# Four weight buffers at four places: 48, 56, 72 and 80 bytes past a multiple of 128, instead of 64 for all

## The chip, the core and the metric

The kernel runs on one core of one Trainium2 chip. The metric is the time of one execution on the device in microseconds (us), the median of several runs. Five engines of the core work side by side and wait for each other through semaphores: TensorE (PE in the profile; its weight loads are listed as PEld), VectorE (DVE), ScalarE (ACT), GpSimd (POOL) and SyncE (SP), which here issues most of the transfers. The on-chip memory has 128 partitions; a tile lies at the same byte address in each of them, and "where a tile lies" below means this address within a partition.

## The reference, cut to what matters

Two layers of a decoder on 256 tokens with a width of 2048, all in float32. Every matrix product of a layer goes through the same piece of code in the kernel:

```python
for i in range(DEPTH):                      # DEPTH = 2
    a = rmsnorm(h, attn_norm[i])
    if i % 2 == 0:                          # 8 stick-breaking and 8 dilated heads
        h = h + sb_dilated_mixer(a, positions, w_in_even[i // 2], w_out_even[i // 2])
    else:                                   # 16 heads with forget gates
        h = h + fox_mixer(a, w_in_odd[i // 2], b_forget[i // 2], w_out_odd[i // 2])
    h = h + conv_ffn(rmsnorm(h, ffn_norm[i]), w_up[i], conv_w[i], conv_b[i], w_down[i])
    gate = sigmoid(rmsnorm(h, ple_norm[i]) @ w_ple_gate[i])
    h = h + gate * (p[i] @ w_ple[i])
return rmsnorm(h, final_norm)
```

The FFN has 5632 hidden features twice (gate and value), so `w_up` and `w_down` are the largest part of the weights.

## The kernel before, in words

All weights lie in the order in which they are used in one long array in the chip's main memory. They are cut into *units*: a unit is up to four k-tiles (128 rows each) of a 256 columns wide stripe of one weight matrix. A list of all units is made ahead (`_units`, L61), and transfers of 1 MB bring two units at a time into one of three raw buffers `wr` (`issue_group`, L150).

A float32 weight is used in two parts. `split_unit` (L169) takes the next unit, ScalarE copies it into a float32r tile as the high part (L176), and VectorE subtracts this high part from the raw value and writes the remainder as the low part (L177). Both parts lie in one tile `w` of 2048 elements per partition, ordered by k-tile, then part, then column. The pool hands out four such buffers in turn (L174). `unit` (L183) keeps three units split ahead (`LOOK = 3`) of the one that TensorE reads.

The activations lie in two large tiles `act` (with high and low part for each k-tile) that change roles, and `pact` for the layer's own embedding. `gemm_unit` (L207) makes 24 matmuls of one unit of four k-tiles: for each of the two 128-column halves, for each k-tile, the three products high x high, high x low and low x high (`PARTS`). The weights are the stationary operand (128 columns, 512 bytes a partition), the activations the moving one (256 tokens, 1024 bytes a partition). For the v projection (`gemm_v`, L240) the roles are exchanged: activations stationary, weights moving. Once, for the second layer's first heads, v and the forget gates are made together, with 272 columns (`gemm_vf`, L253).

The results go to tiles in the accumulation memory named by the product: psq, psk, psv (projections), pso (output projection), psu and psd (FFN up and down), psg (gate), psp (embedding), pse (last gate tile). The attention's own matmuls (`scs`, `sps`, `avp`) are put between the units by a small clock (`tick`, `defer`): a step is due some units after the one that it follows. They read other tiles in plain float32 or, for a few, in float32r.

Where things lie: pools are laid out in the order in which they are opened and used. Ahead of the weight buffers stand `act` twice, `pact` and a tile of 16 elements, `gap` (L117), that nothing reads or writes. The activations begin at a multiple of 128 bytes, and are multiples of 128 long; so the four weight buffers, the raw buffers behind them and `h` and `pl` all begin 64 bytes past a multiple of 128, and the buffers are 8192 bytes apart.

Of the kernel before, what the change touches and what calls it, by code (L numbers as in the profile page):

```python
# [11 lines left out]
F32R = mybir.dt.float32r  # L12
# [5 lines left out]
P = 128  # L18
# [86 lines left out]
def trunk(ctx: ExitStack, tc: tile.TileContext, xT, pT, pos, gains, conv, bf, cst, wst, out):  # L105
# [3 lines left out]
    apool = ctx.enter_context(tc.tile_pool(name="apool", bufs=1))  # L109
    wpool = ctx.enter_context(tc.tile_pool(name="wpool", bufs=1))  # L110
# [3 lines left out]

    bufs = [apool.tile([P, KT, 2, S], F32R, name=f"act{i}") for i in range(2)]
    pact = apool.tile([P, 2, 2, S], F32R, name="pact")
    apool.tile([P, 16], F32, name="gap")  # L117
    h = cpool.tile([P, KT, S], F32, name="h")
    pl = cpool.tile([P, KT, S], F32, name="pl")
# [28 lines left out]
    at = {"group": 0, "off": 0, "unit": 0, "tick": 0, "rows": 0}  # L148

    def issue_group():  # L150
        g = GROUPS[at["group"]]
        n = sum(u[3] * u[5] for u in g)
        if g[0][:2] == ("w_ple", 0):

            op = g[0][4] // 256
            raw = pl[:, 2 * op:2 * (op + len(g)), :].rearrange("p a s -> p (a s)")
        else:
            raw = wpool.tile([P, 2048], F32, name="wr", tag="wr", bufs=3)
        src = wst[at["off"]:at["off"] + P * n].rearrange("(p f) -> p f", p=P)
        nc.sync.dma_start(out=raw[:, :n], in_=src)  # L160
        at["off"] += P * n
        at["group"] += 1
        o = 0
        for u in g:
            m = u[3] * u[5]
            raws.append((u, raw[:, o:o + m].rearrange("p (k c) -> p k c", c=u[5])))
            o += m

    def split_unit():  # L169
        if not raws:  # L170
            issue_group()
        u, raw = raws.pop(0)
        kc, cw = u[3], u[5]
        w = wpool.tile([P, 2048], F32R, name="w", tag="w", bufs=4)  # L174
        w = w[:, :2 * kc * cw].rearrange("p (k s c) -> p k s c", s=2, c=cw)
        nc.scalar.copy(out=w[:, :, 0, :], in_=raw)  # L176
        nc.vector.tensor_sub(out=w[:, :, 1, :], in0=raw, in1=w[:, :, 0, :].bitcast(F32))  # L177
        at["unit"] += 1
        ready.append((u, w))
# [3 lines left out]
    def unit(kind, l, k0, c0):  # L183
        while len(ready) < LOOK and at["unit"] < len(UNITS):
            split_unit()
        u, w = ready.pop(0)
        assert (u[0], u[1], u[2], u[4]) == (kind, l, k0, c0), (u, kind, l, k0, c0)
        return u[3], w
# [458 lines left out]
    for l in range(DEPTH):  # L647
        st = {}
        if l == 0:
            split_unit()  # L650
            rest_of_start()
            for op in range(8):
                if op in (2, 4, 6):
                    for i in (op - 2, op - 1):
                        norm_parts(i, 0, X)
                ple_up(0, op)
            defer(1, lambda: norm_parts(6, 0, X))
            defer(2, lambda: norm_parts(7, 0, X))
            constants()
            for i in range(8):  # L660
                defer(3 + i, lambda i=i: norm_squares(i, tc.keep_in_program_order))
            norm_finish(True, 12, 14)
# [164 lines left out]
```

## Time and profile before

| what | value |
|---|---|
| median of 3 runs | 2423.63 us (2423.62 to 2424.76) |
| the profiled execution's own time | 2424.3 us |
| its span, first to last instruction | 2422.5 us |
| mean granted TensorE clock | 0.997 |
| matmuls in psu (up) and psd (down) | 8448 and 4224 |
| read from main memory | 452.86 MB, 188 GB/s over the span |

The page of the profile gives busy time by engine, the span in 40 slices, the chain of work that ended last, and the costliest groups of instructions. In a group's row stand the line, the engine, the operation, the names of output and inputs, the shapes and the count; then the busy time in us and the mean duration of one in ns; then the idle time of that engine just before them with what ended it. Matmuls are pipelined: one of 276 ns overlaps the next ones, so that the duration isn't the time that a matmul costs. The chain in order of time has rows of three parts, start, length and what ran, and as it has no overlap the length divided by the count is the step from one matmul to the next. The four weight buffers are used in turn, so a piece of 96 matmuls of the chain (one output tile) has gone through each of them once.

### The profile page before, as it was taken

The page shows a single profiled execution, that of the slowest core. Times are in us where ns is not written, and L with a number is a line of the kernel's source. Part 1 is how long each engine was busy: PE and PEld are TensorE (multiplying, and loading weights), DVE is VectorE, ACT ScalarE, POOL GpSimd, SP SyncE. Part 2 cuts the span into 40 slices and gives each one's busy share as a digit, 9 for nine tenths or more (in the row PEclk, how much of TensorE's full clock was granted, in tenths as well). Part 3 has the DMA queues.
Part 4 walks back from the last instruction along what each step waited for, and adds up shares of the span by engine and source line. Part 5 has one row for each costly group of instructions (what it writes and reads, how often), then busy time and mean ns, then how long its engine had stood idle before and what let it go on. Part 6 is the DMA issues. An engine that isn't in the chain of part 4 may idle for free.

```text
span 2422.5 us, 47951 instructions
## 1 busy us (share of the span) xinstructions
PE 2408.5 (99%) x21006; PEld 2403.4 (99%) x21006; DVE 1581.7 (65%) x2066; ACT 1230.9 (51%) x1546; POOL 5.9 (0%) x13
## 2 busy tenths in 40 slices
PE   9999999999999999999999999999999999999998
PEld 9999999999999999999999999999999999999998
DVE  7666766776567657767755555667665776567666
ACT  6654455554355445555554444555544554455554
POOL 0000000000000000000000000000000000000000
PEclk9999999999999999999999999999999999999998
DMA  7444455555555555555555454555555555555553
GB/s 287 170 175 170 175 182 192 192 194 192 197 197 196 187 196 192 193 187 203 185 184 175 167 182 162 198 191 194 192 192 193 194 196 190 202 192 187 187 201 122
DMA packets 66818, 458.05 MB, mean 189 GB/s; under 512 B 7552, under 2 KB 7840, under 8 KB 16944
## 3 DMA queue, kind: packets, MB, share of 16 engines
q1 hardware_dynamic: 66576, 454.93, 53.0%
q8 instruction: 164, 2.69, 0.4%
q14 instruction: 46, 0.38, 0.1%
q0 software_dynamic: 32, 0.06, 0.0%
HBM read 452.86 MB, written 2.10 MB: 188 GB/s over the span
## 4 chain that ended last, share of the span: by engine, by line
PE 99%; DVE 0%; DMA 0%; ACT 0%; issue 0%; SPq 0%; POOLq 0%; DVEq 0%; ACTq 0%
PE psu L214 40%; PE psd L214 20%; PE psk L214 7%; PE psq L214 7%; PE pso L214 7%; PE psv L248 7%; PE psg L214 7%; PE avp L525 1%; PE psv L261 0%; PE psp L214 0%; PE pse L725 0%; PE scs L481 0%; PE sps L516 0%; PE avp L527 0%; DMA h<-in_x 0%; PE scs L479 0%
## 5 line engine op out<-in xcount | busy, mean ns | idle before, releaser
L177 DVE TENSOR_TENSOR w<-wr,w 128x1024 fp32r<-128x1024 f32 (+2 forms) x874 | 1045.9, 1198 | 688.0 <-ACT w L176 683.6
L176 ACT CAST w<-wr 128x1024 fp32r<-128x1024 f32 (+2 forms) x874 | 903.2, 1034 | 1064.2 <-PE psu L214 353.4
L214 PE MATMUL psu<-act,w 128*128 128x256 f32 x8448 | 959.5, 276 | 0.0
L214 PEld LDWEIGHTS psu<-act,w 128*128 128x128 f32 x8448 | 958.3, 188 | 0.0
L214 PE MATMUL psd<-act,w 128*128 128x256 f32 x4224 | 479.7, 276 | 0.0
L214 PEld LDWEIGHTS psd<-act,w 128*128 128x128 f32 x4224 | 479.2, 188 | 0.0
L214 PE MATMUL psk<-act,w 128*128 128x256 f32 x1536 | 183.6, 279 | 0.0
L214 PE MATMUL psq<-act,w 128*128 128x256 f32 x1536 | 182.6, 279 | 0.9 <-DVE w L177 0.9
L214 PEld LDWEIGHTS psq<-act,w 128*128 128x128 f32 x1536 | 178.5, 188 | 1.4 <-DVE w L177 1.1
L214 PEld LDWEIGHTS psk<-act,w 128*128 128x128 f32 x1536 | 179.0, 188 | 0.0
L214 PE MATMUL pso<-act,w 128*128 128x256 f32 x1536 | 176.3, 277 | 0.0
L214 PEld LDWEIGHTS pso<-act,w 128*128 128x128 f32 x1536 | 175.4, 188 | 0.0
L248 PE MATMUL psv<-w,act 128*128 128x256 f32 x1440 | 167.0, 277 | 0.0
L248 PEld LDWEIGHTS psv<-w,act 128*128 128x128 f32 x1440 | 165.1, 188 | 0.1
L214 PE MATMUL psg<-act,w 128*128 128x256 f32 x1440 | 164.6, 276 | 0.0
L214 PEld LDWEIGHTS psg<-act,w 128*128 128x128 f32 x1440 | 163.7, 188 | 0.0
L626 DVE TENSOR_TENSOR u<-psu,rb 128x512 f32<-128x512 f32 x88 | 60.9, 692 | 32.7 <-PE psu L214 32.5
L632 DVE SCALAR_TENSOR_TENSOR yv<-u,cv,yv 128x256 f32<-128x256 f32 x176 | 73.4, 480 | 0.0
L632 DVE SCALAR_TENSOR_TENSOR yg<-u,cv,yg 128x256 f32<-128x256 f32 x176 | 73.4, 480 | 0.0
L629 ACT ACTIVATE yg<-u,cv 128x256 f32<-128x256 f32 x88 | 48.1, 594 | 1.2 <-DVE u L626 1.2
L629 ACT ACTIVATE yv<-u,cv 128x256 f32<-128x256 f32 x88 | 48.0, 594 | 0.0
L272 ACT CAST act<-yg 128x512 fp32r<-128x512 f32 x44 | 27.4, 623 | 38.9 <-DVE yg L642 38.9
(165 smaller groups left out, 887.8 us busy)
## 6 DMA issues: line engine op xcount, KB each, us to landing
wr<-in_w SPq DMA_DIRECT2D x388, 1024.0 KB, 4.8
wr<-in_w SPq DMA_DIRECT2D x36, 768.0 KB, 4.3
wr<-in_w SPq DMA_DIRECT2D x8, 896.0 KB, 4.6
h<-in_x SPq DMA_DIRECT2D x4, 512.0 KB, 8.4
wr<-in_w SPq DMA_DIRECT2D x4, 512.0 KB, 10.2
out_dram<-h SPq DMA_DIRECT2D x7, 256.0 KB, 2.4
wr<-in_w SPq DMA_DIRECT2D x2, 816.0 KB, 4.5
pl<-in_w SPq DMA_DIRECT2D x3, 512.0 KB, 6.9
```

The costliest lines, as they stand in the source:

```text
L176: nc.scalar.copy(out=w[:, :, 0, :], in_=raw)
L177: nc.vector.tensor_sub(out=w[:, :, 1, :], in0=raw, in1=w[:, :, 0, :].bitcast(F32))
L214: nc.tensor.matmul(ps[:, j, :], lhsT=w[:, k, s, js], rhs=act[:, k0 - koff + k, t, :], start=first and j + k + n == 0, stop=last and k == k ...
L248: nc.tensor.matmul(ps[:, t], lhsT=act[:, 4 * i + k, a, tsl], rhs=w[:, k, b], start=i + t + k + n == 0, stop=i == 3 and k == kc - 1 and n = ...
L272: nc.scalar.copy(out=dst[:, :, 0, :], in_=src)
L525: nc.tensor.matmul(av[:, 0, j * S:(j + 1) * S], lhsT=v[:, 0, js], rhs=w[:, j * S:(j + 1) * S], start=j == 0, stop=False, skip_group_check= ...
L626: nc.vector.tensor_mul(out=u[:, :, 2:], in0=ps, in1=rb2)
L629: nc.scalar.activation(out=y[:, j, :], in_=u[:, j, 2:], func=AF.Identity, bias=cv[:, l, t, 3:4], scale=cv[:, l, t, 2:3])
L632: nc.vector.scalar_tensor_tensor(out=y[:, j, :], in0=u[:, j, tap:tap + S], scalar=cv[:, l, t, tap:tap + 1], in1=y[:, j, :], op0=ALU.mult, ...
```

## The change

The four weight buffers are no longer handed out by the pool for every unit. They are four fixed tiles of 2080 elements (8320 bytes, 65 x 128), made behind `pact` and ahead of `gap`, and of each a slice of 2048 elements is used, which begins 12, 14, 18 or 20 elements (48, 56, 72 or 80 bytes) into the tile. Unit n takes the tile n mod 4, the same turn as before. As the tiles begin at a multiple of 128, so the data lie that far past one. The tile `gap` now stands behind them, and what follows is moved up by 512 bytes (4 x 128), which changes nothing in its place within 128 bytes.

```diff
     pact = apool.tile([P, 2, 2, S], F32R, name="pact")
+    wbufs = []
+    for i, past in enumerate((12, 14, 18, 20)):
+        wbufs.append(apool.tile([P, 2080], F32R, name=f"w{i}")[:, past:past + 2048])
     apool.tile([P, 16], F32, name="gap")
...
         kc, cw = u[3], u[5]
-        w = wpool.tile([P, 2048], F32R, name="w", tag="w", bufs=4)
+        w = wbufs[at["unit"] % 4]
         w = w[:, :2 * kc * cw].rearrange("p (k s c) -> p k s c", s=2, c=cw)
         nc.scalar.copy(out=w[:, :, 0, :], in_=raw)
```

## The prediction

> **What bounds the kernel now.** I read the page first, then the chain of waits by line and in order of time, then the groups by shape, and last who waited for whom. The page's first and fourth parts:
>
> ```profile
> span 2422.5 us, 47951 instructions
> PE 2408.5 (99%) x21006; PEld 2403.4 (99%) x21006; DVE 1581.7 (65%) x2066; ACT 1230.9 (51%) x1546; POOL 5.9 (0%) x13
> ...
> PE 99%; DVE 0%; DMA 0%; ACT 0%; issue 0%; SPq 0%; POOLq 0%; DVEq 0%; ACTq 0%
> ```
>
> TensorE alone carries the chain that ended last; VectorE is busy for 65% and ScalarE for 51% beside it. A busy TensorE says little by itself, because matmuls overlap, so what counts is the step from the start of one matmul to the start of the next. The chain in order of time gives it without overlap: each row is the start, the length and the number of matmuls in one unbroken piece.
>
> ```profile
> 127.30 11.31 PE psq L214 x96
> ...
> 237.03 10.89 PE psq L214 x96
> ...
> 1270.12 10.88 PE psv L248 x96
> ...
> 1863.02 152.32 PE psu L214 x1344
> 2015.34 76.16 PE psd L214 x672
> ```
>
> The long FFN pieces divide to 152.32 / 1344 = 113.33 ns and 76.16 / 672 = 113.33 ns; psv, in which the weight buffer is the moving operand and the activations are the stationary one, to 10.88 / 96 = 113.33 ns. Of the two psq tiles of the first layer above, which read the same activations and, as a pair of heads takes 12 units, the same buffers in the same turn, the later takes 10.89 / 96 = 113.4 ns and the earlier 11.31 / 96 = 117.81 ns. So there are two steps, 113.33 and 117.81 ns, which differ by 4.48 ns, and the kernel falls into one or the other. Nearly everything runs at the short one. How much is there to be had from the long one? Its pieces in the chain lie between these two:
>
> ```profile
> 85.56 2.83 PE psv L248 x24
> ...
> 1515.10 5.66 PE pso L214 x48
> ```
>
> They are 33 pieces with 1,224 matmuls in all, each of them starting right behind a block of attention matmuls (scores, transposes, forget-gate sums) and ending by the next such block at the latest, apart from a few matmuls of transition. 1,224 x 4.48 ns = 5.5 us: that is all that the long step costs the kernel before. Behind 1522 us none of length is left; the whole of the second FFN runs at 113.33 ns.
>
> The granted clock gives no room. Its row of the page, in tenths over 40 slices, is at 9 (90% or more) everywhere but in the last:
>
> ```profile
> PEclk9999999999999999999999999999999999999998
> ```
>
> **The change part by part.** The data are the same, the units are the same, and the buffer of unit n is still the (n mod 4)th. What differs is where the four buffers lie: all of them 64 bytes past a multiple of 128 before, and 48, 56, 72 and 80 past afterwards. Three things touch them: ScalarE's copy (L176) and VectorE's subtraction (L177) write them, and TensorE reads them.
>
> The writers first, from the page's costliest groups (count, then busy time and mean ns of one, then idle time before them and what ended most of it) and from the list of who waited for whom (total us, times, longest):
>
> ```profile
> L177 DVE TENSOR_TENSOR w<-wr,w 128x1024 fp32r<-128x1024 f32 (+2 forms) x874 | 1045.9, 1198 | 688.0 <-ACT w L176 683.6
> L176 ACT CAST w<-wr 128x1024 fp32r<-128x1024 f32 (+2 forms) x874 | 903.2, 1034 | 1064.2 <-PE psu L214 353.4
> ```
>
> ```profile
> PE psq L214 <- DVE w L177: 0.9, 1, 0.9
> ```
>
> A unit of 4 k-tiles is 24 matmuls, 24 x 113.33 ns = 2.72 us. The two writers need 1034 + 1198 = 2232 ns one after the other for it in the mean, and they work three units ahead of TensorE, 3 x 2.72 = 8.2 us. In the whole run TensorE waited for a written buffer once by VectorE, for 0.9 us, at the start. So a writer that gets a little slower costs nothing: VectorE idles 2422.5 - 1581.7 = 840.8 us, which is 840.8 / 874 = 0.96 us for each of the 874 subtractions of the page. Only when one subtraction grows by more than that (from 1.20 to 2.16 us) does VectorE become the bound. No row shows a write at another offset; the ends are zero and, if the subtraction doubled, 874 x (1.20 - 0.96) = 210 us more. A gain is excluded, since TensorE doesn't wait for the writers. I take zero, because only a growth by four fifths would be felt at all, and put 2 in 100 on the other end.
>
> The bookkeeping of the buffers comes next. A tile that the pool hands out anew for each unit becomes one of four fixed tiles. ScalarE's copy still waits for the matmuls that read that buffer four units earlier, the row above names these waits (353.4 us on psu alone), and nothing else is queued that TensorE needs: the releaser is TensorE itself. If the wait came two matmuls sooner or later, it would move a copy by 0.2 us under a cover of 8.2 - 2.2 = 6.0 us. Cost: nothing. The other tiles move by whole multiples of 128 bytes (each of the four takes 8,320 bytes instead of 8,192, and 4 x 128 = 512), so they keep their place within 128 bytes. Transfers into the raw buffers keep their sizes and their order on SP's queue.
>
> That leaves TensorE's reads, and they are the whole case. The matmuls that read these buffers are, from part 5 of the page:
>
> ```profile
> L214 PE MATMUL psu<-act,w 128*128 128x256 f32 x8448 | 959.5, 276 | 0.0
> L214 PE MATMUL psd<-act,w 128*128 128x256 f32 x4224 | 479.7, 276 | 0.0
> L214 PE MATMUL psk<-act,w 128*128 128x256 f32 x1536 | 183.6, 279 | 0.0
> L214 PE MATMUL psq<-act,w 128*128 128x256 f32 x1536 | 182.6, 279 | 0.9 <-DVE w L177 0.9
> L214 PE MATMUL pso<-act,w 128*128 128x256 f32 x1536 | 176.3, 277 | 0.0
> L248 PE MATMUL psv<-w,act 128*128 128x256 f32 x1440 | 167.0, 277 | 0.0
> L214 PE MATMUL psg<-act,w 128*128 128x256 f32 x1440 | 164.6, 276 | 0.0
> ```
>
> Together 8448 + 4224 + 3 x 1536 + 2 x 1440 = 20,160. One nanosecond on each is 20.2 us, so that a change of the step by 0.24 ns already shows. What do the rows say of an offset? For "no effect": psq stands at 113.4 and at 117.81 ns with one and the same placement, so the place of the data doesn't decide alone between the two; what ran just ahead does. And psv, with the operands' places exchanged (moving data at 64, stationary at 0), takes exactly the step of psu. For "some effect" there is one row, the combined v and forget-gate product, whose units have rows of 272 columns, 1,088 bytes, so that its reads fall by turns 64 and 0 bytes past a multiple of 128:
>
> ```profile
> 1189.95 16.09 PE psg L214 x142
> 1206.04 6.73 PE psv L261 x54
> ```
>
> 6.73 / 54 = 124.6 ns for 272 columns is 0.458 ns a column. The short step is 113.33 / 256 = 0.443, the long one 117.81 / 256 = 0.460. So the one place where the buffers are read at mixed offsets runs at about the long rate, though not behind attention work: the gate product just before it has the short one, 16.09 / 142 = 113.3 ns. It may be the width that does it, and not the place; this trace can't part the two. The bounds for one matmul are therefore from 4.48 ns less (for those now at the long step) to 4.48 ns more (for those at the short one). I take zero for the sum, which is nearest to the two psq rows and to psv: 2424.3 us for the profiled execution (its span of 2422.5 and 1.8 around it), and, as that execution is 0.7 us above the median of the runs, 2423.6 us.
>
> **The rivals.** *The mixed offsets end the long pieces* (faster). A long piece goes on from matmul to matmul at a fixed rhythm until a block of other work breaks it. If that rhythm depends on how the weight's place stands to the activation's, then a new offset every unit would break it within one unit of 24. For it: the two steps are sharply separate and each holds on, as a rhythm would; a short one has held for 1344 matmuls. Against it: 11.31 us for 96 passes through four buffers without leaving, and nothing in the rows ties the rhythm to places. All 33 pieces gone is 5.5 us, 2418.1; half of them gone is 2420.9, which still counts as no change. There is a further end of the same side: the shortest step that the chain shows for any 128-wide weight load is that of the transposes,
>
> ```profile
> 1259.95 0.66 PE sps L516 x6
> ```
>
> 0.66 / 6 = 110 ns, and if some of the offsets let the main matmuls come down to it, all four would give 20,160 x 3.33 + 5.5 = 72.6 us less, 2351. No row of these shapes is below 113.33, so that gets little. [...]
>
> *Some offsets force the long step* (slower). The mechanism: TensorE fetches a weight row of 128 values and a moving row of 256 values at once, and the place of one against the other decides how often they meet. At 64 they meet little enough for 113.33 ns; in the units whose buffer is badly placed each matmul takes 117.81. For it: the 272-column row above. Against it: psv with the roles exchanged, and the equal psd and psu pieces. If two of the four buffers are bad, (20,160 - 1,224) / 2 x 4.48 ns = 42.4 us come on top: 2466.0. One bad buffer gives 2444.8, four give 2508. It decides from the first buffer in four whose units run more than 0.95 ns longer per matmul (4.8 us / 5,040).
>
> [...]
>
> *The writers become late* (slower, with its price above) is left with 2 in 100.
>
> **How the numbers follow.** 0.2% of the time, 4.8 us, is about what a measurement of this kernel can tell from no change. No effect on the step, or only on part of the long pieces: 0.40, and this is the forecast, 2423.6. Faster by more than that: 0.24, of which 0.16 for the end of nearly all long pieces at about 2418 and 0.08 for a shorter main step. Slower: 0.36, of which 0.10 for a fraction of the long step's surcharge or one bad buffer (up to 2445), 0.14 for two bad buffers by the long step or by the extra line (2459 to 2466), 0.10 for three or four, and 0.02 for the writers. I put the low end at 2417, just under the end of the long pieces, which leaves out the 0.08; the high end at 2467 just over two bad buffers, which leaves out 0.12. The forecast's own range, with some of the long pieces moved either way, is 2420 to 2427.
>
> **What would show it.** Right: the FFN pieces of the chain still divide to 113.33 ns (152.3 us for 1344), the weights' groups keep 276 ns and 188 ns as means of one, and the psq and psk pieces of 24 to 96 matmuls still come in two lengths. The first rival: no piece with 2.83 us for 24 is left between 85 and 1515 us, with the FFN unchanged. The second: the step changes every 24 matmuls with the buffer, the psu piece of 1344 is above 152.3 us (up to 1344 x 117.81 ns = 158.3 if all four are bad), and the windows of the FFN count fewer matmuls in 100 us. The writers' case: VectorE's groups on the buffers are near 2.2 us, and TensorE has idle time released by them. The forecast is wrong if the FFN's step is not 113.33 in every buffer, or if the long pieces vanish as a whole.

## The result, and the profile after

The changed kernel takes 2511.23 us (median of 4 runs, 2510.09 to 2511.86), the kernel before 2424.2 us beside it. The ratio is 1.0356, with a 95% interval of 1.0343 to 1.0369: slower by 87 us. The forecast was no change, and the range ended at 2467.

The page of the kernel after, first and fourth part, answers to the same lines of before:

```profile
span 2510.0 us, 48176 instructions
PE 2495.1 (99%) x21006; PEld 2490.0 (99%) x21006; DVE 1582.5 (63%) x2066; ACT 1227.6 (49%) x1546; POOL 5.8 (0%) x13
...
PE 99%; DVE 0%; DMA 0%; ACT 0%; issue 0%; SPq 0%; POOLq 0%; DVEq 0%; ACTq 0%
```

By these lines nothing has happened but that TensorE is busy for 87 us longer. VectorE and ScalarE do the same work in the same time (1582.5 against 1581.7, 1227.6 against 1230.9), there are as many matmuls, and TensorE still holds the whole chain. The granted clock hasn't fallen either: its mean over the span is 0.998 now and was 0.997 before. The writers' groups confirm that they play no part:

```profile
L180 DVE TENSOR_TENSOR w<-wr,w 128x1024 fp32r<-128x1024 f32 (+2 forms) x874 | 1046.3, 1198 | 729.3 <-ACT w L179 725.5
L179 ACT CAST w<-wr 128x1024 fp32r<-128x1024 f32 (+2 forms) x874 | 899.8, 1030 | 1164.3 <-PE psu L217 388.9
```

1198 and 1030 ns a piece, against 1198 and 1034: in the mean over the four new places a write costs what it cost at 64, and both engines idle a little more (729.3 us where it was 688.0, 1164.3 where it was 1064.2), since TensorE releases the buffers later (388.9 us of ScalarE's idle time end with psu alone, 353.4 before).

It is the step that shows it, from the chain in order of time (start, length, what ran):

```profile
32.08 11.30 PE psk L217 x96
43.38 11.48 PE psv L251 x96
...
684.74 158.25 PE psu L217 x1344
842.98 79.13 PE psd L217 x672
```

158.25 / 1344 = 117.75 ns where it was 113.33; psv, in which the weights are the moving operand, 11.48 / 96 = 119.6. There are no two kinds of pieces any more: all are long. The sum closes: 18,936 matmuls that ran at the short step x 4.42 ns = 83.7 us, and 1,440 in psv x 1.85 ns on top = 2.7, together 86.4 of the 87.5 us by which the span grew.

Does one of the four buffers do it, or all? The chain cut to one unit each, four units of one psd tile in a row, with the data at 48, 56, 72 and 80 (four pieces, each cut to the stretch of one unit, so that 23 steps lie in it):

```profile
594.31 2.71 PE psd L217 x23
```

```profile
597.14 2.71 PE psd L217 x23
```

```profile
599.96 2.72 PE psd L217 x23
```

```profile
602.81 2.69 PE psd L217 x23
```

A unit at the short step would read 23 x 113.33 ns = 2.61. All four are long. Over all units of the FFN the mean steps are 117.8, 117.9, 118.5 and 116.9 ns.

### The profile page after: what moved, and what is told of

Read it like the earlier page. It is cut to its first block, busy times and chain, and to the rows that moved or that the text cites. A ratio compares the mean times of both kernels' runs of the same rounds, so it can differ in the third digit from the quotient of the medians.

```text
span 2510.0 us, 48176 instructions
## 1 busy us (share of the span) xinstructions
PE 2495.1 (99%) x21006; PEld 2490.0 (99%) x21006; DVE 1582.5 (63%) x2066; ACT 1227.6 (49%) x1546; POOL 5.8 (0%) x13
## 4 chain that ended last, share of the span: by engine, by line
PE 99%; DVE 0%; DMA 0%; ACT 0%; issue 0%; SPq 0%; POOLq 0%; DVEq 0%; ACTq 0%
PE psu L217 40%; PE psd L217 20%; PE psq L217 7%; PE psk L217 7%; PE pso L217 7%; PE psv L251 7%; PE psg L217 7%; PE avp L528 1%; PE psv L264 0%; PE psp L217 0%; PE pse L728 0%; PE scs L484 0%; PE sps L519 0%; DMA h<-in_x 0%; PE avp L530 0%; PE scs L482 0%
## 5 line engine op out<-in xcount | busy, mean ns | idle before, releaser
L180 DVE TENSOR_TENSOR w<-wr,w 128x1024 fp32r<-128x1024 f32 (+2 forms) x874 | 1046.3, 1198 | 729.3 <-ACT w L179 725.5
L179 ACT CAST w<-wr 128x1024 fp32r<-128x1024 f32 (+2 forms) x874 | 899.8, 1030 | 1164.3 <-PE psu L217 388.9
L217 PE MATMUL psu<-act,w 128*128 128x256 f32 x8448 | 996.7, 280 | 0.0
L217 PEld LDWEIGHTS psu<-act,w 128*128 128x128 f32 x8448 | 995.4, 188 | 0.0
L217 PE MATMUL psd<-act,w 128*128 128x256 f32 x4224 | 498.4, 280 | 0.0
L217 PEld LDWEIGHTS psd<-act,w 128*128 128x128 f32 x4224 | 497.8, 188 | 0.0
L217 PE MATMUL pso<-act,w 128*128 128x256 f32 x1536 | 182.3, 280 | 0.0
L251 PE MATMUL psv<-w,act 128*128 128x256 f32 x1440 | 175.2, 282 | 0.0
L251 PEld LDWEIGHTS psv<-w,act 128*128 128x128 f32 x1440 | 173.2, 189 | 0.1
L217 PE MATMUL psg<-act,w 128*128 128x256 f32 x1440 | 170.8, 280 | 0.0
L217 PEld LDWEIGHTS psg<-act,w 128*128 128x128 f32 x1440 | 169.9, 188 | 0.0
L271 DVE TENSOR_TENSOR h<-h,psd 128x512 f32<-128x512 f32 x48 | 33.0, 687 | 18.5 <-PE psd L217 18.5
```

Of the source, the lines that this page charges most:

```text
L217: nc.tensor.matmul(ps[:, j, :], lhsT=w[:, k, s, js], rhs=act[:, k0 - koff + k, t, :], start=first and j + k + n == 0, stop=last and k == k ...
L251: nc.tensor.matmul(ps[:, t], lhsT=act[:, 4 * i + k, a, tsl], rhs=w[:, k, b], start=i + t + k + n == 0, stop=i == 3 and k == kc - 1 and n = ...
L271: nc.vector.tensor_add(out=hs, in0=hs, in1=ps)
```

## The experiments

After the result three theories stood. *Distance*: the place of the weights against the activations sets the step, buffer by buffer, and each of the four new places is bad. *Mixture*: any place will do so long as it stays the same from unit to unit. *Bookkeeping*: it is not the place at all. The change has a second side to it that the diff hides: with fixed tiles 1,748 matmuls carry a semaphore increment in the trace after, where there were 950 (presumably because the waits for the high and the low part are then tracked apart).

**Fixed tiles at 64, and the offsets without the tiles.** The first run keeps the change and undoes the offsets:

```diff
-    for i, past in enumerate((12, 14, 18, 20)):
+    for i, past in enumerate((16, 16, 16, 16)):
```

> The four fixed tiles of the changed kernel, with the data of all four 64 bytes past a multiple of 128: the change's bookkeeping (fixed tiles 8320 bytes apart, and 1748 matmuls that carry a semaphore increment where there were 950) without its offsets. If each buffer's own offset sets the step, or if the mixture of offsets does: 2424 us, the FFN step back at 113.3 ns. If the bookkeeping does it: 2511 us, step 117.7 ns.

The second keeps the pool and makes the offsets in it (its buffers begin at 64, so that 28, 30, 2 and 4 elements more give 48, 56, 72 and 80):

```diff
+        past = (28, 30, 2, 4)[at["unit"] % 4]
-        w = wpool.tile([P, 2048], F32R, name="w", tag="w", bufs=4)
-        w = w[:, :2 * kc * cw]
+        w = wpool.tile([P, 2080], F32R, name="w", tag="w", bufs=4)
+        w = w[:, past:past + 2 * kc * cw]
```

> The pool of the kernel before, and in it the data 48, 56, 72 and 80 bytes past a multiple of 128: the offsets without the bookkeeping. Own offset or mixture: 2511 us, step 117.7 ns. Bookkeeping: 2424 us, step 113.3 ns.

Measured, in one execution each: 2429.05 us for the fixed tiles at 64, and 2511.21 us for the pool with offsets (2425.56 for the kernel before, beside both). The FFN's piece of 1344 in the chain, first with the fixed tiles, then in the pool:

```profile
663.82 152.32 PE psu L217 x1344
```

```profile
684.17 158.29 PE psu L215 x1344
```

Bookkeeping falls: the offsets alone make the whole difference, the tiles alone none in the FFN. The 3.5 us that the fixed tiles at 64 cost lie in the v products (psv), in which the weights are the moving operand. A tile of them reads

```profile
116.68 11.11 PE psv L251 x96
```

where the kernel before has 10.88: 11.11 / 96 = 115.7 ns instead of 113.33, and 1,440 x 2.4 ns = 3.5 us. Some of these units are short and some long (113.4 to 118.0 ns). The buffers stand 8,320 instead of 8,192 bytes apart in this kernel, and more matmuls carry increments; whether either of these does it was not tried.

**One buffer at 48, and four at 0, 32, 64 and 96.** These two tell distance from mixture.

```diff
-    for i, past in enumerate((12, 14, 18, 20)):
+    for i, past in enumerate((16, 16, 16, 12)):      # and (0, 8, 16, 24)
```

> Three fixed tiles at 64 and the fourth at 48. If each buffer's own offset sets the step of its units: a quarter of the units goes from 113.3 to 117.7 ns, 5,040 x 4.4 ns = 22 us, 2446 us, and the step changes with the unit. If a constant placement from unit to unit is what holds the short step: nearly all units long, 2500 us or more. If 48 by itself is harmless and it takes several offsets: 2424 us.

> The four fixed tiles at 0, 32, 64 and 96. Own offset: the units of the buffer at 64 are at 113.3 ns, those of the other three at whatever theirs is, so between 2424 us (multiples of 32 are all good) and 2490 us (three quarters long). Mixture: 2511 us and no unit short, not even those at 64.

Measured: 2483.2 and 2502.16 us. The first fits none of its three numbers, and the units say why. One psd tile of it, units at 64, 64, 64 and 48:

```profile
586.51 2.71 PE psd L217 x23
```

```profile
589.33 2.71 PE psd L217 x23
```

```profile
592.16 2.61 PE psd L217 x23
```

```profile
594.88 2.72 PE psd L217 x23
```

The unit at 48 is long, but so are the two at 64 that come behind it; only the third finds back. So the long step is carried on into units at 64, where the short one, 2.61 us, also runs, just as behind attention in the kernel before (2.83 us for 24 in psv). In the second run, units at 0, 32, 64 and 96:

```profile
591.81 2.76 PE psd L217 x23
```

```profile
594.68 2.76 PE psd L217 x23
```

```profile
597.55 2.61 PE psd L217 x23
```

```profile
600.28 2.68 PE psd L217 x23
```

This run is over the 2490 us that own offsets were given, which rested on 117.7 ns for the three others, and 0 and 32 are longer than that. The unit at 64 is short at once, although its neighbours differ: 2.61 / 23 = 113.5, between 2.76 / 23 = 120.0 and 2.68 / 23 = 116.5. Mixture falls: a change of place from unit to unit doesn't forbid the short step. Distance stands, with an addition: at 64 both steps are possible (2.71 and 2.61 us for 23 in the run with one buffer at 48), and which one runs goes with what ran ahead: there the first two units behind the one at 48 are long, the third is short.

**All at 56, the neighbourhood of 64, and the activations moved.** The first two are again a line of offsets, (14, 14, 14, 14) and (13, 15, 17, 19).

> All four fixed tiles at 56. If each buffer's own offset sets the step, as the units at 48, 32 and 96 suggest: every FFN matmul near the 117.9 ns that the units at 56 have in the changed kernel, 2424 + 20,160 x 4.5 ns = 2515 us. If a constant placement is what lets the short step hold: 2424 to 2430 us and 113.3 ns.

> Fixed tiles at 52, 60, 68 and 76. Own offset, and a short step that is there only at 64 itself: no unit at 113.3 ns, 2505 to 2520 us. Own offset with a short step in a small zone about 64: the units at 60 and 68 short, half of the matmuls, about 2470 us.

The other two leave the weights' own place and change the activations', by moving the 64 unused bytes ahead of them; `swapped` makes the same move in the kernel with fixed tiles at 64, by which these come to lie at a multiple of 128:

```diff
+    apool.tile([P, 16], F32, name="gap")
     bufs = [apool.tile([P, KT, 2, S], F32R, name=f"act{i}") for i in range(2)]
     pact = apool.tile([P, 2, 2, S], F32R, name="pact")
-    apool.tile([P, 16], F32, name="gap")
```

> The kernel before with its 64 unused bytes ahead of the activations instead of behind them: the weight buffers stay 64 past a multiple of 128, the activations go from 0 to 64 past one. If what counts is the weights' place in itself: 2424 us, step 113.3 ns. If it is the distance between weights and activations (now 0): the 119.8 ns that the units at 0 have in the run with 0, 32, 64 and 96, 2424 + 20,160 x 6.5 ns = 2555 us.

> Activations at 64 and the four fixed weight tiles at 0: the distance is still 64, the other way round. If the distance counts: 2424 to 2430 us, as with fixed tiles at 64. If the weights' place in itself counts: 2555 us, step 119.8 ns.

Measured (kernel before 2425.2 us): all at 56, 2511.76; near 64, 2484.85; activations at 64, 2553.4; swapped, 2431.85, a little over the 2430 expected. The pieces of the chain, all at 56, then weights and activations both at 64, then swapped:

```profile
684.05 158.29 PE psu L217 x1344
```

```profile
694.59 161.28 PE psu L214 x1344
```

```profile
664.46 152.32 PE psu L217 x1344
```

The middle one is the strongest of all. Not one byte of the weight buffers has moved in it, they lie at 64 as before, and each matmul takes 161.28 / 1344 = 120.0 ns; with the weights at 0 and the activations at 64 it is 113.33 again. So, in these products with the weights stationary, the distance between the two operands counts, and not the place of either. And a constant 56 is as long as a mixed one: 158.29 / 1344 = 117.8 ns, where the units at 56 in the changed kernel have 117.9.

The run near 64 missed both expectations. Its units at 52, 60, 68 and 76:

```profile
589.29 2.61 PE psd L217 x23
```

```profile
592.01 2.73 PE psd L217 x23
```

```profile
594.85 2.72 PE psd L217 x23
```

```profile
597.69 2.61 PE psd L217 x23
```

Not the nearest ones are short, 60 and 68, but those 12 bytes off.

**52 and 76 for all, and the rest of the circle.** With (13, 13, 13, 13), (19, 19, 19, 19), (7, 10, 22, 25) and (4, 11, 21, 28).

> All four fixed tiles at 52, where the units of the run with 52, 60, 68 and 76 were short. If 52 is as good a distance as 64: FFN step 113.3 ns, 2424 to 2432 us, with long pieces behind attention as at 64. If 52 has no long rhythm at all: 2419 us, faster than the kernel before by 0.2%. If it was short only because its neighbour in turn was at 76: about 2512 us.

> All four fixed tiles at 76, the same question on the other side of 64: 2424 to 2432 us as at 64, 2419 us without long pieces, about 2512 us if it needs its neighbour.

> Fixed tiles at 28, 40, 88 and 100, which lie 24 and 36 bytes from 64, as 52 and 76 lie 12. If the short step recurs every 12 bytes: all units short, 2424 to 2432 us. If it stays within 12 bytes of 64: all long, 2495 to 2560 us by the 116.5 to 120 ns seen outside.

> Fixed tiles at 16, 44, 84 and 112, to see whether any distance gives a step under 113.3 ns. If 113.3 is a floor that distances can only raise: 2480 to 2560 us and no unit under 113.3. If the floor belongs to the distance 64: some unit below it, down to the 110 ns of the transposes.

Measured: 2434.45 us with all at 52 (ratio 1.004, 1.0025 to 1.0055), 2 us over the end of what was expected, 2431.74 with all at 76 (1.0029, 1.0018 to 1.0039); the scans 2516.93 and 2530.63. In both kernels with one distance the FFN's piece of 1344 has 152.32 us. So 52 and 76 allow the short step, 113.33 ns, on their own, where the weights are the stationary operand. Where they are the moving one, in psv, they don't. A tile of the run at 52, then of that at 76:

```profile
118.14 11.68 PE psv L251 x96
```

```profile
117.21 11.31 PE psv L251 x96
```

That is 121.7 and 117.8 ns a matmul, where the kernel before has 113.33. Over 1,440 matmuls it makes 12.0 and 6.5 us, and the two kernels are 9.7 and 7.0 us slower than the one before. The long pieces behind attention are not the reason: counting matmul by matmul, outside psv 846 steps (at 52) and 832 (at 76) are over 114 and under 126 ns, where the kernel before has 1,401. So a distance that is good with the weights stationary need not be good with the roles exchanged.

In the scans no place gives the short step for good. The mean step within the units of the FFN (weights stationary), by the distance of their buffer from the activations, over the runs in which it was tried:

| bytes | step, ns | bytes | step, ns |
|---|---|---|---|
| 0 | 120.0 | 64 | 113.4 (116.0 in the run with one buffer at 48) |
| 16 | 118.3 | 68 | 118.4 |
| 28 | 117.1 | 72 | 118.5 |
| 32 | 119.9 | 76 | 113.6 (114.4 in the run near 64) |
| 40 | 120.1 | 80 | 116.9 |
| 44 | 118.9 | 84 | 120.0 |
| 48 | 118.0 | 88 | 116.7 |
| 52 | 113.4 | 96 | 116.7 |
| 56 | 117.8 | 100 | 119.8 |
| 60 | 118.4 | 112 | 118.7 |

The long pieces of the kernels with one of the three good distances divide to 113.33. No mean is under 113.33.

**Without the writers, and the good distances mixed.** What the table doesn't tell is who meets whom: the shifted buffers are written by ScalarE and VectorE while TensorE reads others. So two kernels stop writing after 32 units, the changed one and that with fixed tiles at 64; TensorE goes on reading the old contents.

```diff
-        nc.scalar.copy(out=w[:, :, 0, :], in_=raw)
-        nc.vector.tensor_sub(out=w[:, :, 1, :], in0=raw, in1=w[:, :, 0, :].bitcast(F32))
+        if at["unit"] < 32:
+            nc.scalar.copy(out=w[:, :, 0, :], in_=raw)
+            nc.vector.tensor_sub(out=w[:, :, 1, :], in0=raw, in1=w[:, :, 0, :].bitcast(F32))
```

> The changed kernel (48, 56, 72, 80), which leaves out the splitting of all units but the first 32: ScalarE and VectorE don't write the buffers any more, TensorE reads the same old contents through the same addresses, the transfers go on. If the long step comes from TensorE's own two reads: the FFN stays at 117.7 ns, 2508 to 2512 us. If it comes from the writers' shifted writes: 113.3 ns, 2418 to 2430 us.

> The four fixed tiles at 64, with the same part left out. Beside it the run above is read: 113.3 ns in the FFN and 2418 to 2430 us by either explanation; a step below 113.3 ns would say that the writers cost something at every distance.

Measured: 2510.54 and 2429.87 us. The chain of the first, then of the second:

```profile
684.06 158.25 PE psu L218 x1344
```

```profile
664.84 152.32 PE psu L218 x1344
```

With two engines taken off the buffers neither step moves by a hundredth of a nanosecond (158.25 and 152.32 as with them). So the writers don't make the long step. With the run in which only the activations moved (120.0 ns instead of 113.33), that leaves, by exclusion, TensorE's own two reads, of its weights and of its moving operand; no run shows these reads themselves. The last run has the offsets (13, 16, 19, 16):

> Fixed tiles at 52, 64, 76 and 64, a new distance for every unit, and each of the three allows the short step by itself. If a change of distance ends a long piece within a unit: the pieces behind attention shrink from 1,224 matmuls to a few hundred at most, 2419 to 2421 us. If the short step doesn't survive the changes: 2440 us or more. If neither: 2425 to 2434 us, as with one distance for all.

Measured: 2431.06 us, ratio 1.0026 (1.0015 to 1.0037). Neither expectation of an effect came true. In the FFN the short step survives a change among the three good distances from unit to unit (152.32 us for 1344 again), and the long pieces behind attention don't end by it: outside psv 1,312 steps are over 114 and under 126 ns, against 1,529 with all fixed tiles at 64 and 1,401 in the kernel before. The 6.2 us over the kernel before are again those of psv: most of its tiles take 11.28 us for 96, and 1,440 x 4.2 ns = 6.0 us. No kernel tried is faster than the one before.

## Why the prediction was wrong, step by step

**The bound and the lever were right.** TensorE's step carries the time, 20,160 matmuls of about 113 ns, and the prediction priced a nanosecond of it at 20 us. The time after is that price.

**The step that failed is the choice of zero for TensorE's reads.** It rested on this: "psq stands at 113.4 and at 117.81 ns with one and the same placement, so the place of the data doesn't decide alone between the two; what ran just ahead does." The row is right, and the conclusion from it holds only at 64. It shows that the place is not enough to fix the step; it doesn't show that another place allows the short step too. With the weights stationary, both a short and a long step occur at one and the same distance: at 64 2.61 and 2.71 us for 23 (the run with one buffer at 48), at 52 152.32 us for 1344 and 5.72 for 48 (a piece of psq, 119.2 ns), at 76 152.32 us and 2.94 for 24 (a piece of psk, 122.5 ns). There the place leaves both open; at 0 or 56 the short one wasn't there to be had (120.0 and 117.8 ns in the long pieces). In place of zero, all four new distances are long, 116.9 to 118.5 ns, and that makes 86 of the 87 us. One placement in the trace can't tell "the place has no effect" from "this place is one of the few good ones". The psv row, taken as a second support, could not either: exchanging the roles turns a distance of 64 into 128 - 64 = 64, the very same. Elsewhere psv does not take the step of psu: at 52 it is at 121.7 ns, and psu at 113.33.

**The second rival was right in what decides, and nearly so in its price.** It named the place of the weight row against the moving row, and that is what the runs show: with only the activations moved, the step goes from 113.33 to 120.0 ns. That the two fetches meet, as it also said, no run shows; it was the author's guess. It gave 2508 us for four bad buffers; measured 2511.23. That it came so near is luck in part: it took 117.81 ns, the long step at 64, for the step of any bad place, and the four chosen ones happen to lie around it, while others reach 120. It had 0.10 for three or four bad buffers, and the range was closed at two. Nothing in the profile spoke for two rather than four; two was the author's estimate. The extra line, from which the forecast has its 2459 for two bad buffers, is a term that no run shows. In its place the runs showed the four offsets nearly alike in the FFN (117.8, 117.9, 118.5 and 116.9 ns at 48, 56, 72 and 80), and the short step, 113.33, at 52 and 76. The bound for one matmul, 4.48 ns more, was too low as well: at a distance of 0 it is 120.0 - 113.33 = 6.7 ns. The long step of the trace was the nearest row, but no ceiling.

**The one row that spoke for an effect was right in sign.** The 272-column product, read at 64 and 0 by turns, ran at the long rate (6.73 us for 54, 0.458 ns a column). Whether the place or the width does it there wasn't tried.

**The other steps.** The writers at nothing: right, their durations are unchanged (1198 and 1030 ns), and without them the step stays (158.25 us for 1344). The bookkeeping at nothing: right for the change as made (2511.21 without it, 2511.23 with it). The first rival, that mixed offsets end the long pieces: wrong even among good distances (1,312 steps over 114 ns outside psv, where the kernel before has 1,401). A step of 110 ns: not seen as the mean of any of 20 distances, the lowest being 113.4, nor in a long piece (113.33).

What stays open is why three distances 12 bytes apart are good; why a unit at 64 stays long for two units behind one at 48, and not behind one at 32; and why psv, with the roles exchanged, is long at 52 and 76, and in part with fixed tiles at 64 though not in the pool.

## What to carry to other kernels

In this kernel, which TensorE bounds with back-to-back pairs of weight load and matmul, the distance between the stationary and the moving tile within 128 bytes moved the time by up to 5% (2553.4 us at 0, 2425.2 at 64). In another kernel of this kind it is worth trying, like a tile size, and for each role of a tile: here 52 is good for weights that are stationary (113.33 ns), and the worst tried with one distance for weights that move (121.7 ns). An edit that did no more than move 64 unused bytes took the step from 113.33 to 120.0 ns, so read the step (length over count of a long piece of the chain) before and after, and not the busy share, which was 99% before and after. And a state that comes and goes at one setting says nothing about another setting: to price a placement, look for a row with another placement, and if there is none, give the range the worst step for all of the matmuls.

## What the runs showed of the hardware that was not expected

- The step of a float32r pair (128 x 128 weights, 256 moving columns) is 113.33 ns in the long FFN pieces at distances of 52, 64 and 76 bytes, and in the FFN's units 116.7 to 120.1 ns in the mean at the 17 other distances tried, 120.0 at 0.
- With the weights stationary it is the distance that counts: weights 64 and activations 0, or weights 0 and activations 64, 152.32 us for 1344 matmuls each; both at 64, 161.28 us.
- The roles count too: with the weights moving, 96 matmuls take 11.68 us at 52 and 11.31 us at 76, where they take 10.88 us at 64 in the kernel before.
- Whether two engines write the other weight buffers, or stop after the first 32 units, makes no difference to either step (158.25 and 158.25 us, 152.32 and 152.32 us for 1344).
- The long rhythm outlived its cause here: behind a unit at 48 two units at 64 run at 2.71 us for 23 matmuls, and the third at 2.61.
